# The last feature tiles in slices of 384 and 128 tokens, the closing norm applied over four tiles at a time

## The chip, the cores and the metric

The kernel runs on one core of a Trainium2 chip. The metric is device time in microseconds (us), the median of three runs. Lower is better.

## What is computed

Two transformer-like blocks over 512 tokens and 1024 features. Only the last step matters here, the second convolutional feed-forward of the second block, whose output passes a root-mean-square norm and is added to the residual:

```python
def rms_norm(x, g):
    xf = x.astype(jnp.float32)
    y = xf * lax.rsqrt(jnp.mean(xf * xf, axis=-1, keepdims=True) + EPS)
    return (y * g.astype(jnp.float32)).astype(x.dtype)
...
def conv_ffn(h, w_up, w_conv, b_conv, w_down):
    g, u = jnp.split(h @ w_up, 2, axis=-1)
    g = causal_dwconv(g, w_conv) + b_conv.astype(g.dtype)
    return (jax.nn.silu(g) * u) @ w_down
...
        x = x + rms_norm(conv_ffn(h, w_up[layer], w_ffn_conv[layer], b_ffn_conv[layer], w_down[layer]),
                         norm_g[layer, 3])
```

## The kernel before

Features lie on the 128 partitions, tokens along the free axis, so the residual is eight feature tiles `X[0]` to `X[7]` of 128x512. Each float32 product is made of three matmuls in the fp32r format (`mm3`, lines 175 to 177): a high and a low part of the weights (`whi`, `wlo`) against a high and a low part of the activations (`mh`, `ml`). `wload` brings a block of weights of up to 1024 columns by DMA into `raw`, ScalarE makes `whi` of it (line 137), VectorE makes `wlo` as the difference (line 144). There are three buffers of each.

The down projection of a feed-forward is done by `finish`: for each of the eight output tiles 22 blocks of weights, so 66 matmuls and three weight loads (1024, 1024 and 768 columns). Tiles 0 to 5 are done over all 512 tokens. The last `split` tiles (two here, 6 and 7) are done in two slices of tokens, `HALVES`: tiles 6 and 7 for tokens 0 to 255, then tiles 7 and 6 for tokens 256 to 511. The weights of tile 7 are kept for the second slice, those of tile 6 are loaded and split again. After each tile `evac` multiplies the result by a per-token factor `R` into `mix` (line 476, VectorE) and collects its squares (`stat`): ScalarE squares, VectorE adds to `acc` (lines 265 and 266); the last tile of a slice goes another way, its squares (line 255) are summed on TensorE directly (`sums`, line 283, one matmul for every 128 tokens).

After each slice comes `after(c)`, that is `post`: `rnorm` makes the factor of the norm from the sums in small operations (lines 298 to 305; the square root needs a table load on ScalarE), spreads it over the partitions by matmuls into PSUM (line 308), and then for each of the eight feature tiles one VectorE operation multiplies `mix` by the norm's weight and factor (line 383), one adds it to the residual (line 385; in the last slice four of the eight adds are on GpSimd), and SyncE issues the output's DMA (line 394). The first slice's `post` lies beside the second slice's matmuls, the second one's is the end of the kernel.

The order of the instructions on each engine is settled when the program is built. Engines work through their own list in order and wait on each other by semaphores. TensorE's weight loads (PEld) run beside its matmuls.

Of the kernel before, what the change touches and what calls it, by code (L numbers as in the profile page):

```python
# [9 lines left out]
F32 = mybir.dt.float32  # L10
F32R = mybir.dt.float32r
AF = mybir.ActivationFunctionType
ALU = mybir.AluOpType
# [3 lines left out]
P = 128  # L17
S = 512
D = 1024
KD = D // P  # L20
# [12 lines left out]
HALVES = (slice(0, S // 2), slice(S // 2, S))  # L33
# [16 lines left out]
class Net:  # L50
# [164 lines left out]
        for (key, _), p in zip(tiles, ps):  # L215
            self.ready[key] = p

    def finish(self, src, acts, split, evac, after, pool=None):


        K = len(acts)
        n = KD - split
        for m in range(n):
            evac(m, self.proj(src[m], acts, "mo"[m % 2], key=("out", m)), WHOLE)
        if not split:
            return after(WHOLE)
        alloc = None
        if pool is not None:
            alloc = lambda: [[pool.tile([P, 1024], F32R, name=nm, tag="w", bufs=2 * split)] for nm in ("oh", "ol")]
        chunks = [range(k0, min(K, k0 + 8)) for k0 in range(0, K, 8)]  # L230
        load = lambda m: [self.wload(src[m][:, ks[0] * P : ks.stop * P], alloc) for ks in chunks]
        w = {m: load(m) for m in range(n, KD)} if pool is not None else {}
        i = 0
        for c in HALVES:
            ms = range(n, KD) if c.start == 0 else range(KD - 1, n - 1, -1)
            for m in ms:
                wm = w[m] if m in w else load(m)
                if m == KD - 1:
                    w[m] = wm
                ps = self.psum("mo"[i % 2])[:, 0 : S // 2]  # L240
                i += 1
                for ks, wc in zip([self.order] if self.order else chunks, wm):
                    self.mmk(ps, wc, acts, ks, c, ks[0] if self.order else 0, ks[-1] if self.order else K - 1)
                evac(m, ps, c, m == ms[-1])
            after(c)


    def stat(self, t, c, first, of="x", direct=False):

        nc = self.nc  # L250
        if direct:
            sq = self.tp.tile([P, S // 2], F32, name="sq", tag="sq", bufs=2)
            for h in HALVES:
                if c.start <= h.start < c.stop:
                    nc.scalar.activation(sq, t[:, h], AF.Square)
                    self.sums(sq, h, c, of)
            return
        if first and c.start == 0:
            self.acc[of] = self.tp.tile([P, S], F32, name="acc", tag="acc", bufs=1)
        acc = self.acc[of]  # L260
        if first:
            nc.scalar.activation(acc[:, c], t[:, c], AF.Square)
        else:
            sq = self.tmp("sq")
            nc.scalar.activation(sq[:, c], t[:, c], AF.Square)
            nc.vector.tensor_tensor(out=acc[:, c], in0=acc[:, c], in1=sq[:, c], op=ALU.add)
# [110 lines left out]
    def post(self, mix, gname, g0, nxt, c):  # L377

        nc = self.nc
        R = self.rnorm("mix", D, None, c)  # L380
        for k in range(KD):
            t = mix[k][:, c]
            nc.vector.scalar_tensor_tensor(t, t, self.vec(gname, g0 + k), R[:, c], ALU.mult, ALU.mult)
            eng = nc.gpsimd if nxt[0] == "end" and c.stop == S and k < 6 and k % 3 < 2 else nc.vector
            eng.tensor_tensor(out=self.X[k][:, c], in0=self.X[k][:, c], in1=t, op=ALU.add)
            if nxt[0] == "normed":
                if k % 2:
                    self.stat2(self.X[k - 1 : k + 1], c)
            elif nxt[0] == "scaled":
                if k == 0 and c.start == 0:  # L390
                    self.alloc_h()
                self.h_scaled(nxt, k, c)
            else:
                nc.sync.dma_start(self.out[k][:, c], self.X[k][:, c])
        if nxt[0] == "scaled":
            for k in range(0, KD, 2):
                self.stat2(self.X[k : k + 2], c)

    def first_begin(self, tiles, allocs):

# [22 lines left out]
    def ffn(self, up, down, nxt, conv=None, post=None, extra=None):  # L423
        nc, tc = self.nc, self.tc
        with tc.tile_pool(name="mida", bufs=KD) as sa, tc.tile_pool(name="mid", bufs=2 * KF - KD) as sp:
            with tc.tile_pool(name="ft", bufs=2) as fp:
                part = lambda nm: [sp.tile([P, S], F32R, name=nm, tag="s") for _ in range(2)]
                tiles = [((up.tensor.name, i), up[i]) for i in range(6)]
                allocs = [lambda: (part("bh"), part("bl"))] * 3
                if self.early:  # L430
                    self.begin(tiles, allocs)
                else:
                    self.first_begin(tiles, allocs)
                    self.early = True
                R = self.R
                if conv is not None:
                    pads = [fp.tile([P, S + 2], F32, name=f"pad{i}", bufs=1) for i in range(2)]
                    for t in pads:
                        nc.gpsimd.memset(t[:, 0:2], 0.0)
                mids = []  # L440
                h = self.H
                for j in range(KF):
                    pg = self.proj(up[2 * j], h, "m", key=(up.tensor.name, 2 * j))
                    pu = self.proj(up[2 * j + 1], h, "o", key=(up.tensor.name, 2 * j + 1))
                    gp = fp.tile([P, S], F32, name="gp", tag="gp")
                    if conv is None:
                        nc.vector.tensor_tensor(out=gp, in0=pg, in1=R, op=ALU.mult)
                    else:
                        wn, bn, l = conv
                        pad = pads[j % 2]  # L450
                        nc.vector.tensor_tensor(out=pad[:, 2:], in0=pg, in1=R, op=ALU.mult)
                        w = lambda t: self.vec(wn, (l * 3 + t) * KF + j)
                        nc.scalar.activation(gp, pad[:, 2:], AF.Identity, bias=self.vec(bn, l * KF + j), scale=w(2))
                        nc.vector.scalar_tensor_tensor(gp, pad[:, 1 : S + 1], w(1), gp, ALU.mult, ALU.add)
                        nc.vector.scalar_tensor_tensor(gp, pad[:, 0:S], w(0), gp, ALU.mult, ALU.add)
                    nc.scalar.activation(gp, gp, AF.Silu)
                    md = fp.tile([P, S], F32, name="md", tag="md")
                    nc.vector.tensor_tensor(out=md, in0=pu, in1=gp, op=ALU.mult)  # L458
                    mids.append(self.split(sa if j < KD // 2 else sp, md, "s", "m"))
                    if extra is not None:  # L460
                        gen, steps = extra
                        for _ in range(steps * (j + 1) // KF - steps * j // KF):
                            next(gen, None)
            with tc.tile_pool(name="fm", bufs=KD) as mp:
                mix = {}

                def evac(m, ps, c, last=False):
                    if post is None:
                        t = self.tmp("dx")
                        nc.vector.scalar_tensor_tensor(t[:, c], ps, 0.5, R[:, c], ALU.mult, ALU.mult)  # L470
                        nc.vector.tensor_tensor(out=self.X[m][:, c], in0=self.X[m][:, c], in1=t[:, c], op=ALU.add)
                        self.updated(nxt, m, c, last)
                    else:
                        if m not in mix:
                            mix[m] = mp.tile([P, S], F32, name="mix", tag="mix")
                        nc.vector.tensor_tensor(out=mix[m][:, c], in0=ps, in1=R[:, c], op=ALU.mult)
                        self.stat(mix[m], c, m == 0, "mix", last)

                def after(c):
                    if post is not None:  # L480
                        self.post(mix, *post, nxt, c)
                    self.prep(nxt, c)

                self.finish(down, mids, 3 if nxt[0] == "normed" else 2, evac, after)


    def attention(self, ap, Q, K, V, blocks, step, logits, out, mask=None, lag=1, bank=None):
# [843 lines left out]
```

## Time and profile before

| | |
|---|---|
| median of 3 runs (2466.15 to 2467.6) | 2467.29 us |
| the profiled execution's own time | 2469.19 us |
| its span | 2467.4 us |
| TensorE busy | 2403.5 us, 97% of the span |
| VectorE, ScalarE, GpSimd busy | 1468.1, 1129.9, 39.1 us |
| mean granted TensorE clock | 0.992 of full speed |

The profile is of one execution, whose span is 1.8 us shorter than its own time. A row of windows gives a stretch (start:end, its length), then the busy time and the number of instructions (x) of PE, PEld, DVE, ACT and POOL, the granted TensorE clock as a share of full speed, and the DMA engines' share and rate. Names in rows are those of the program, with buffer numbers left out. PE is TensorE's matmuls, PEld its weight loads, DVE VectorE, ACT ScalarE, POOL GpSimd, SPq the DMA queue of SyncE.

### The profile page before, as it was taken

How to read it: one execution, taken by the hardware profiler on the slowest of the kernel's cores; microseconds unless marked ns; L12 is line 12 of the kernel's file. 1: busy time of each engine (PE TensorE's matmuls, PEld its weight loads, DVE VectorE, ACT ScalarE, POOL GpSimd, SP SyncE). 2: the span in 40 equal slices, each digit the busy share in tenths (PEclk: the TensorE clock that was granted, in tenths of full speed). 3: DMA queues.
4: the chain of work that ended last, by engine and by line, in shares of the span. 5: the costliest groups of instructions: out<-in, count | busy, mean ns of one | idle time of the engine just before them, and what ended most of it. 6: DMA issues, size and time to landing. Idle time of an engine off the chain costs nothing.

```text
span 2467.4 us, 32211 instructions
## 1 busy us (share of the span) xinstructions
PE 2403.5 (97%) x12710; PEld 2048.5 (83%) x12710; DVE 1468.1 (60%) x2524; ACT 1129.9 (46%) x1849; POOL 39.1 (2%) x75
## 2 busy tenths in 40 slices
PE   9999999999999999999999999999999979999998
PEld 8888898777777798888988798888898859888887
DVE  5444347888888755553556665554357996555524
ACT  5223236766666544442355554333246566433322
POOL 0000000000000000000000000000001120000000
PEclk9999999999999999999999999999999999999999
DMA  4232333322222256663432222322344413223233
GB/s 151 94 102 92 94 112 119 95 88 88 80 99 84 86 204 213 214 227 95 117 118 82 85 94 69 102 95 90 101 151 150 145 53 136 69 97 101 90 96 94
DMA packets 83559, 276.08 MB, mean 112 GB/s; under 512 B 9328, under 2 KB 14064, under 8 KB 83408
## 3 DMA queue, kind: packets, MB, share of 16 engines
q1 hardware_dynamic: 83408, 274.03, 34.4%
q8 instruction: 99, 1.62, 0.3%
q14 instruction: 52, 0.43, 0.1%
HBM read 257.20 MB, written 16.80 MB: 111 GB/s over the span
## 4 chain that ended last, share of the span: by engine, by line
PE 84%; DVE 9%; ACT 4%; issue 2%; DMA 1%; POOL 0%; SPq 0%; ACTq 0%; DVEq 0%; POOLq 0%
PE psm L177 15%; PE psm L175 15%; PE psm L176 15%; PE pso L176 10%; PE pso L175 10%; PE pso L177 10%; DVE wlo L144 1%; DVE pso L1063 1%; ACT whi L137 1%; PE pst L516 1%; PE pso L532 1%; PE pst L175 1%; PE pst L176 1%; PE pst L283 1%; PE pst L177 1%
## 5 line engine op out<-in xcount | busy, mean ns | idle before, releaser
L137 ACT CAST whi<-raw 128x1024 fp32r<-128x1024 f32 (+3 forms) x402 | 408.5, 1017 | 770.3 <-issue 340.3
L144 DVE TENSOR_TENSOR wlo<-raw,whi 128x1024 fp32r<-128x1024 f32 (+2 forms) x380 | 447.7, 1179 | 311.0 <-ACT whi L137 309.9
L175 PE MATMUL psm<-hh,whi 128*128 128x512 f32 (+1 forms) x1512 | 573.2, 380 | 4.2 <-ACT hh L326 3.0
L177 PE MATMUL psm<-hl,whi 128*128 128x512 f32 (+1 forms) x1512 | 569.0, 377 | 0.1
L176 PE MATMUL psm<-hh,wlo 128*128 128x512 f32 (+1 forms) x1512 | 569.0, 376 | 0.0
L175 PEld LDWEIGHTS psm<-hh,whi 128*128 128x128 f32 x1512 | 285.7, 189 | 54.1 <-ACT hh L326 3.9
L177 PEld LDWEIGHTS psm<-hl,whi 128*128 128x128 f32 x1512 | 285.7, 189 | 49.7 <-DVE hl L327 0.7
L176 PEld LDWEIGHTS psm<-hh,wlo 128*128 128x128 f32 x1512 | 286.2, 189 | 46.5
L175 PE MATMUL pso<-hh,whi 128*128 128x512 f32 (+1 forms) x728 | 272.8, 375 | 0.9 <-ACT whi L137 0.9
L176 PE MATMUL pso<-hh,wlo 128*128 128x512 f32 (+1 forms) x728 | 272.4, 374 | 0.2 <-DVE wlo L144 0.2
L177 PE MATMUL pso<-hl,whi 128*128 128x512 f32 (+1 forms) x728 | 272.5, 374 | 0.0
L176 PE MATMUL psm<-mh,wlo 128*128 128x512 f32 (+1 forms) x506 | 172.5, 341 | 1.6 <-DVE wlo L144 1.6
L175 PE MATMUL psm<-mh,whi 128*128 128x512 f32 (+1 forms) x506 | 172.1, 340 | 0.0
L177 PE MATMUL psm<-ml,whi 128*128 128x512 f32 (+1 forms) x506 | 172.0, 340 | 0.0
L458 DVE TENSOR_TENSOR md<-pso,gp 128x512 f32<-128x512 f32 x84 | 58.0, 692 | 169.7 <-PE pso L177 168.2
L175 PEld LDWEIGHTS pso<-hh,whi 128*128 128x128 f32 x728 | 137.9, 189 | 25.1 <-ACT whi L137 1.1
L176 PEld LDWEIGHTS pso<-hh,wlo 128*128 128x128 f32 x728 | 137.9, 189 | 24.3 <-DVE wlo L144 0.4
L177 PEld LDWEIGHTS pso<-hl,whi 128*128 128x128 f32 x728 | 137.8, 189 | 24.5 <-issue 0.5
L176 PE MATMUL pso<-mh,wlo 128*128 128x256 f32 (+1 forms) x440 | 145.7, 331 | 1.3 <-DVE wlo L144 1.3
L175 PE MATMUL pso<-mh,whi 128*128 128x256 f32 (+1 forms) x440 | 145.9, 332 | 0.3 <-ACT whi L137 0.3
L177 PE MATMUL pso<-ml,whi 128*128 128x256 f32 (+1 forms) x440 | 145.8, 331 | 0.0
L176 PEld LDWEIGHTS psm<-mh,wlo 128*128 128x128 f32 x506 | 96.8, 191 | 12.6 <-DVE wlo L144 2.2
(293 smaller groups left out, 3763.5 us busy)
## 6 DMA issues: line engine op xcount, KB each, us to landing
raw<-w_up SPq DMA_DIRECT2D x88, 512.0 KB, 3.3
raw<-w_ffn_gu SPq DMA_DIRECT2D x87, 512.0 KB, 3.4
raw<-w_in SPq DMA_DIRECT2D x56, 512.0 KB, 3.3
raw<-w_ffn_down SPq DMA_DIRECT2D x40, 512.0 KB, 3.5
raw<-w_in_odd SPq DMA_DIRECT2D x40, 512.0 KB, 3.9
raw<-w_down SPq DMA_DIRECT2D x38, 512.0 KB, 3.5
raw<-w_in_even SPq DMA_DIRECT2D x24, 512.0 KB, 3.6
w_in_odd_lo<-raw SPq DMA_DIRECT2D x20, 512.0 KB, 3.0
```

What stands on the lines that cost most here:

```text
L137: nc.scalar.copy(hi, raw[:, c])
L144: nc.vector.tensor_tensor(out=lo, in0=raw[:, c], in1=hi.bitcast(F32), op=ALU.subtract)
L175: nc.tensor.matmul(out, w[0], x[0], start=start, stop=False)
L176: nc.tensor.matmul(out, w[1], x[0], start=False, stop=False)
L177: nc.tensor.matmul(out, w[0], x[1], start=False, stop=stop)
L283: self.nc.tensor.matmul(st[:, b : b + 1], sq[:, i * P : (i + 1) * P], self.ones[:, 0:1], start=new and i == 0, stop=True, skip_group_check ...
L458: nc.vector.tensor_tensor(out=md, in0=pu, in1=gp, op=ALU.mult)
L516: nc.tensor.transpose(pt[:, i * P : (i + 1) * P], p[:, i * P : (i + 1) * P], self.ident)
L532: nc.tensor.matmul(o[:, q0:q1], V[:, g, a].rearrange("p i d -> p (i d)"), p[:, c], start=first, stop=g == 3 and p is pl, skip_group_check= ...
L1063: nc.vector.scalar_tensor_tensor(t, pad[:, i : i + S], w(i), t, ALU.mult, ALU.add)
```

## The change

For the last feed-forward alone (`end`), the two slices become tokens 0 to 383 and 384 to 511. `mix` becomes one tile `MA` of 128x8x512, so that an operation can run over four feature tiles. The norm's weight is multiplied in by ScalarE right after a tile's squares are taken, and `post_end` takes the place of `post`: for each group of four tiles one multiplication by the norm's factor, one addition to the residual, and one output transfer, all on VectorE and SyncE.

```diff
-    def finish(self, src, acts, split, evac, after, pool=None):
+    def finish(self, src, acts, split, evac, after, pool=None, cuts=HALVES):
...
-        for c in HALVES:
+        for c in cuts:
...
-                ps = self.psum("mo"[i % 2])[:, 0 : S // 2]
+                ps = self.psum("mo"[i % 2])[:, 0 : c.stop - c.start]
...
-            for h in HALVES:
-                if c.start <= h.start < c.stop:
-                    nc.scalar.activation(sq, t[:, h], AF.Square)
-                    self.sums(sq, h, c, of)
+            for h in (slice(a, min(a + S // 2, c.stop)) for a in range(c.start, c.stop, S // 2)):
+                nc.scalar.activation(sq[:, : h.stop - h.start], t[:, h], AF.Square)
+                self.sums(sq, h, c, of)
...
-            eng = nc.gpsimd if nxt[0] == "end" and c.stop == S and k < 6 and k % 3 < 2 else nc.vector
-            eng.tensor_tensor(out=self.X[k][:, c], in0=self.X[k][:, c], in1=t, op=ALU.add)
+            nc.vector.tensor_tensor(out=self.X[k][:, c], in0=self.X[k][:, c], in1=t, op=ALU.add)
...
-            else:
-                nc.sync.dma_start(self.out[k][:, c], self.X[k][:, c])
...
+    def post_end(self, mix, c):
+
+        nc = self.nc
+        n = c.stop - c.start
+        R = self.rnorm("mix", D, None, c)[:, c].rearrange("p (k s) -> p k s", k=1).to_broadcast([P, 4, n])
+        out = self.out.rearrange("k p s -> p k s")
+        for k in range(0, KD, 4):
+            t, x = (a[:, k : k + 4, c] for a in (mix, self.XA))
+            nc.vector.tensor_tensor(out=t, in0=t, in1=R, op=ALU.mult)
+            nc.vector.tensor_tensor(out=x, in0=x, in1=t, op=ALU.add)
+            nc.sync.dma_start(out[:, k : k + 4, c], x)
...
+                        nc.vector.tensor_tensor(out=t[:, c], in0=ps, in1=R[:, c], op=ALU.mult)
+                        self.stat(t, c, m == 0, "mix", last)
+                        if end:
+                            nc.scalar.activation(t[:, c], t[:, c], AF.Copy, scale=self.vec(post[0], post[1] + m))
...
+                cuts = (slice(0, 3 * P), slice(3 * P, S)) if end else HALVES
+                self.finish(down, mids, 3 if nxt[0] == "normed" else 2, evac, after, cuts=cuts)
```

Ahead of the last feed-forward's down projection the order of instructions is the same on every engine. Three places show what moves.

The first is VectorE's list from the last step of the first slice's norm factor (`r`) to the last `wlo` of the second slice. Before:

```order
L305 SCALAR_TENSOR_TENSOR r<-y,r 128x2 [waits DVE_49]
L144 TENSOR_TENSOR wlo<-raw,whi 128x1024 [waits DMAHW3_49,Activation_49]
L383 SCALAR_TENSOR_TENSOR mix<-mix,vecs,pst 128x256 [waits PE_49]
L383 SCALAR_TENSOR_TENSOR mix<-mix,vecs,pst 128x256
L385 TENSOR_TENSOR x<-x,mix 128x256 [waits DVE_49] x2
...
L476 TENSOR_TENSOR mix<-psm,R 128x256 [waits PE_49]
L144 TENSOR_TENSOR wlo<-raw,whi 128x1024 [waits DMAHW4_49,Activation_49]
L266 TENSOR_TENSOR acc<-acc,sq 128x256 [waits Activation_49]
L144 TENSOR_TENSOR wlo<-raw,whi 128x768 [waits DMAHW5_49]
```

The same stretch of the change:

```order
L304 SCALAR_TENSOR_TENSOR r<-y,r 128x3 [waits DVE_49]
L403 TENSOR_TENSOR mix<-mix,pst 128x4x384 [waits PE_49]
L403 TENSOR_TENSOR mix<-mix,pst 128x4x384
L404 TENSOR_TENSOR x<-x,mix 128x4x384 [waits DVE_49] x2
L144 TENSOR_TENSOR wlo<-raw,whi 128x1024 [waits DMAHW3_49,Activation_49]
L144 TENSOR_TENSOR wlo<-raw,whi 128x1024 [waits DMAHW4_49,Activation_49]
L486 TENSOR_TENSOR mix<-psm,R 128x128 [waits PE_49]
L144 TENSOR_TENSOR wlo<-raw,whi 128x768 [waits DMAHW5_49,Activation_49]
```

Sixteen operations of 256 tokens (the dots stand for twelve of them) become four of 4x384, and the first `wlo` for tile 6 of the second slice stood ahead of them and now stands behind them.

The second is ScalarE's list from the square of the first slice's last tile to the first `whi` of tile 6 in the second slice. Before:

```order
L255 ACTIVATE sq<-mix 128x256 [waits DVE_49]
L299 ACT_TABLE_LOAD
L299 ACTIVATE u<-pst,epst 128x2 [waits DVE_49]
L137 CAST whi<-raw 128x1024 [waits DMAHW3_49,PE_49,Activation_49]
```

The same stretch of the change:

```order
L254 ACTIVATE sq<-mix 128x256 [waits DVE_49]
L254 ACTIVATE sq<-mix 128x128 [waits PE_49]
L489 ACTIVATE mix<-mix,vecs 128x384 [waits Activation_49]
L298 ACT_TABLE_LOAD
L298 ACTIVATE u<-pst,epst 128x3 [waits DVE_49]
L137 CAST whi<-raw 128x1024 [waits DMAHW3_49,PE_49]
```

A second square, which waits for TensorE to have read the first out of the same buffer, and the multiplication by the norm's weight now stand ahead of the table load.

The third is VectorE's list behind the last tile of the kernel. Of the change, from the first step of the norm factor on:

```order
L297 TENSOR_SCALAR v<-pst 128x1 [waits PE_49]
L299 RECIPROCAL r<-u 128x1 [waits Activation_49]
L303 SCALAR_TENSOR_TENSOR y<-r,v 128x1 [waits DVE_49]
L304 SCALAR_TENSOR_TENSOR r<-y,r 128x1 [waits DVE_49]
L403 TENSOR_TENSOR mix<-mix,pst 128x4x128 [waits PE_49]
L403 TENSOR_TENSOR mix<-mix,pst 128x4x128
L404 TENSOR_TENSOR x<-x,mix 128x4x128 [waits DVE_49] x2
```

Before, eight multiplications and four additions of 128x256 stood there on VectorE, with four additions on GpSimd, and two operations `y` in place of the one. On TensorE the 66 matmuls of a tile stay 66, of 384 columns in the first slice and of 128 in the second.

## Rows read from the trace of the kernel before

**Rows 1.** The page, first part: busy time (share) and instructions; fourth part: chain by engine.
```profile
PE 2403.5 (97%) x12710; PEld 2048.5 (83%) x12710; DVE 1468.1 (60%) x2524; ACT 1129.9 (46%) x1849; POOL 39.1 (2%) x75
...
PE 84%; DVE 9%; ACT 4%; issue 2%; DMA 1%; POOL 0%; SPq 0%; ACTq 0%; DVEq 0%; POOLq 0%
```
**Rows 2.** Busy time by windows: first slice, second slice, what follows the last matmul.
```profile
2420.38:2436.21 15.83, 15.83 (x134) 15.83 (x132) 6.33 (x8) 4.62 (x6) 0.00 (x0) 1.00 0.47 145
2436.21:2455.21 19.00, 17.74 (x146) 17.24 (x144) 10.98 (x27) 5.31 (x7) 0.00 (x0) 1.00 0.17 57
...
2455.21:2467.40 12.19, 1.74 (x12) 1.49 (x12) 6.30 (x18) 0.68 (x2) 2.96 (x4) 0.69 0.26 86
```
**Rows 3.** Timeline (start, us, what): fp32r matmuls of 384 columns, four in a row.
```profile
490.47 0.34 PE L532 MATMUL pso<-ph,v 128*128 128x384 f32 x1
...
491.00 0.34 PE L532 MATMUL pso<-pl,v 128*128 128x384 f32 x1
```
**Rows 4.** Timeline: fp32r matmuls of 128 columns and their weight loads, one after another.
```profile
1917.88 0.22 PE L532 MATMUL pso<-ph,v 128*128 128x128 f32 x1
...
1917.94 0.27 PE L532 MATMUL pso<-pl,v 128*128 128x128 f32 x1
1917.99 0.19 PEld L502 LDWEIGHTS pst<-kh,qs 128*128 128x128 f32 x1
1918.05 0.28 PE L502 MATMUL pst<-kh,qs 128*128 128x128 f32 x1
...
1918.33 0.19 PEld L175 LDWEIGHTS psm<-hh,whi 128*128 128x128 f32 x1
```
**Rows 5.** Chain of waits, then timeline: VectorE in the second slice, TensorE's stall.
```profile
2442.68 0.78 DVE mix L383 x2
2443.47 0.67 DVE x L385 x2
...
2448.84 1.14 DVE wlo L144
...
2450.02 0.39 PE L176 MATMUL pso<-mh,wlo 128*128 128x256 f32 x1 [1.25 <-DVE wlo L144]
```
**Rows 6.** Timeline: VectorE's evacuation of 512 tokens, ScalarE behind the first slice.
```profile
2420.58 0.69 DVE L476 TENSOR_TENSOR mix<-pso,R 128x512 f32<-128x512 f32 x1 [1.73 <-PE pso L177]
...
2436.87 0.42 ACT L255 ACTIVATE sq<-mix 128x256 f32<-128x256 f32 x1 [7.22 <-DVE mix L476]
2437.30 1.28 ACT L299 ACT_TABLE_LOAD   x1
```
**Rows 7.** Chain of waits behind the last matmul (start, us, what).
```profile
2455.24 0.43 DVE mix L476
...
2456.16 1.07 PE pst L283 x8
...
2457.94 0.36 DVE y L304 x2
...
2458.64 0.70 PE pst L308 x4
2459.36 1.66 DVE mix L383 x4
...
2464.01 0.42 DVE x L385
```
**Rows 8.** DMA issues: count, KB each, median us from issue to landing.
```profile
raw<-lru_w SPq DMA_DIRECT2D x8, 256.0 KB, 2.7
...
out<-x SPq DMA_DIRECT2D x16, 128.0 KB, 1.8
```
**Rows 9.** TensorE's timeline at an earlier norm, and the window behind it.
```profile
1490.63 0.61 PE L283 MATMUL pst<-ones,sq 128*128 128x1 f32 x4 [1.20 <-DVE sq L273]
1492.66 0.68 PE L308 MATMUL pst<-spread,r 128*128 128x128 f32 x4 [1.42 <-DVE r L305]
...
1494.00:1497.40 3.40, 3.40 (x18) 3.40 (x17) 3.05 (x5) 2.80 (x3) 0.00 (x0) 0.51 0.02 6
```

More of the change, by code (lines that the diff above doesn't have):

```diff
@@ L463, in ffn @@
                             next(gen, None)
-            with tc.tile_pool(name="fm", bufs=KD) as mp:
-                mix = {}
+            with tc.tile_pool(name="fm", bufs=1) as mp:
+                end = nxt[0] == "end"
+                if post is not None:
+                    MA = mp.tile([P, KD, S], F32, name="mix")
+                    mix = [MA[:, m, :] for m in range(KD)]
                 def evac(m, ps, c, last=False):
@@ L473, in evac @@
                     else:
[L474 to L477, printed above, removed]
+                        t = mix[m]
+                        nc.vector.tensor_tensor(out=t[:, c], in0=ps, in1=R[:, c], op=ALU.mult)
+                        self.stat(t, c, m == 0, "mix", last)
+                        if end:
+                            nc.scalar.activation(t[:, c], t[:, c], AF.Copy, scale=self.vec(post[0], post[1] + m))
                 def after(c):
+                    if end:
+                        return self.post_end(MA, c)
                     if post is not None:
@@ L482, in after @@
                     self.prep(nxt, c)
-                self.finish(down, mids, 3 if nxt[0] == "normed" else 2, evac, after)
+                cuts = (slice(0, 3 * P), slice(3 * P, S)) if end else HALVES
+                self.finish(down, mids, 3 if nxt[0] == "normed" else 2, evac, after, cuts=cuts)
     def attention(self, ap, Q, K, V, blocks, step, logits, out, mask=None, lag=1, bank=None):
```

## Prediction

> **What bounds the kernel now.** I read the page first: TensorE is busy for 97% of the span and carries 84% of the chain that ended last [rows 1], so whatever TensorE takes longer for goes into the time unless it was waiting anyway. Then the end, by windows [rows 2]. The first slice takes 15.83 us for its 132 matmuls of 256 columns, 0.120 us each, with TensorE never idle. The second takes 19.00 us from its first matmul to the end of its last: 15.84 us of matmuls at that rate, some 1.4 us of the norm's small ones (twelve between the matmuls), and a stall of 1.25 us, in which TensorE waits for a `wlo` that stands behind the first slice's norm on VectorE [rows 5]. From there to the end of the span are 12.19 us, a chain of short steps on VectorE, ScalarE and TensorE, 5.07 us of norm and residual (2459.36 to 2464.43) and 2.97 us of output transfer [rows 7, 2]. So the change touches three stretches: two bound by TensorE, one by latency. I take them in turn, and call F the start of the second slice.
>
> **First slice, 256 to 384 columns.** Four fp32r matmuls of 384 columns with a weight load each start 0.53 us apart over three gaps, 0.173 to 0.180 us each with the rounding of the starts [rows 3]; I take 0.175. 132 of them are 23.1 us, against 15.83: **+7.3 us**. Nothing hides it, since TensorE has no idle time there.
>
> **Second slice, 256 to 128 columns.** A matmul is not cheaper in proportion. Among matmuls of 128 columns, one whose weights were loaded early starts 0.06 us after the one before it (1917.88 to 1917.94), but the next comes 0.11 later, and the weight loads of such a run follow each other at (1918.33 - 1917.99)/3 = 0.113 us [rows 4]. In a steady run the weight load sets the pace, because every matmul has its own. The bounds are 0.06 and 0.113; I take 0.113, the row of a run. So the second slice's matmuls come to 132 x 0.113 = 14.9 us, only 0.9 less than now: the columns saved here do not pay for those added in the first slice.
>
> The Trainium skill, "TensorE: Matmul & The Clock Gate", section on the back-to-back issue gap, gives about 81 ns per matmul for a stream of weight loads and matmuls of 128 columns. No run here shows that figure; the measured 0.113 is higher. By the page's figure the 65 matmuls that count below would take 2.1 us less, and the sum would be so much lower, still a loss.
>
> But matmuls are not all that sets this slice. The steps, each from its start: the evacuation of 384 tokens begins at F+0.20 as now and takes 0.56 us (half way between 0.43 for 256 and 0.69 for 512 [rows 7, 6]); the square of 256 tokens 0.42 [rows 6], to F+1.2; two sums on TensorE, which the second square must wait for, some 0.6; that square of 128 tokens about 0.32 (between half of 0.42 and all of it), to F+2.2; then on ScalarE the multiplication by the norm's weight, 0.53 (between 0.42 and 0.63 if it goes by the columns), and the table load of 1.28 [rows 6], to F+4.05. Before, the table load stood right behind the square and was hidden by the sums. Square root, reciprocal, three `y` at 0.18 and the last step take the factor to F+5.3 and its spreading on TensorE, six matmul instructions at 0.113 plus the wait for the last, to F+6.35. TensorE has work for part of that: 21 matmuls stand ahead of the spreading, and some 1.6 us are waits.
>
> Now VectorE runs the four wide operations, and the first `wlo` of tile 6 behind them. An operation on 256 tokens costs 0.39 us at line 383 and 0.335 at line 385 [rows 5], and 256 more tokens 0.26 more (0.69 less 0.43). 1536 elements are six such parts: 0.39 + 5 x 0.26 = 1.69 and 1.64, for four 6.65 us. Bounds: 6.2 if only the slope counts, 8.7 if each part pays its full price; I take 6.65, since the 512-token row shows the slope. They end at F+13.0, and the `wlo` (1.14 [rows 5]) at F+14.2. TensorE has done the other 45 matmuls of tile 7 by F+11.2 and one of tile 6, then waits **3.0 us**, against 1.25 now. From there 65 matmuls at 0.113 take 7.4 us, and the next two `wlo`, due at F+15.3 and about F+16.5, come before they are needed at F+16.9 and F+19.6. The last evacuation starts at F+21.75, against F+19.03: **+2.7 us**.
>
> **The clock.** The rows of an earlier norm show what such waits can do: TensorE was idle 1.20 and then 1.42 us within some three us, and the granted clock of the next 3.4 us was 0.51 [rows 9], which is the lower of its levels (1.2 against 2.4 GHz). In the second slice of before, with one wait of 1.25 us, it stayed at 1.00 [rows 2]. A wait of 3.0 us is longer than both together, so I expect one fall as long as that. While it lasts the work goes at half speed, so 3.4 us cost up to 1.7; part falls into the wait itself. I take **+1.4 us**, with bounds of 0 (no fall) and about 4.5 (half speed for most of tile 6 and of the small matmuls behind it).
>
> **What follows the last matmul.** Evacuation -0.13 (half the slope), square -0.10, sums four instructions instead of eight, -0.5 of 1.07, one `y` instead of two -0.18, spreading two instead of four -0.23 of 0.70 [rows 7]. The norm and residual: four operations of 512 elements, 0.65 and 0.60 each, 2.5 us instead of 5.07: -2.55. In sum -3.7. The last transfer is 256 KB instead of 128: the nearest rows are 2.7 and 1.8 us to landing [rows 8], +0.9 (from 0, if only the latency counts, to 1.8, if it queues behind its twin, issued 0.6 us earlier). **-2.8 us**, between -3.7 and -1.9.
>
> ScalarE's eight multiplications by the norm's weight cost nothing ahead of the slices: it is busy 4.62 of 15.83 us in the first slice [rows 2]. Uncovered, each would cost up to 0.6. GpSimd's four adds go without loss, since they lay beside VectorE's. No weight load is queued behind the wide transfers: all are issued before.
>
> **Sum.** 7.3 + 2.7 + 1.4 - 2.8 = +8.6 us. The profiled execution would go from a span of 2467.4 to 2476.0, and its time from 2469.19 to 2477.8; that execution is 1.9 us above the median of the runs, 2467.29, which becomes **2475.9**, 0.35% slower. A measurement of this kernel tells differences from about 0.2%, 4.9 us.
>
> **The rivals.**
> - *The clock holds.* Same mechanism without the fall: +7.2, 2474.5. For it: it stayed up over the wait of 1.25 us. Against it: what followed a little less idle time than 3.0 us in [rows 9]. 0.25.
> - *The clock stays low for longer,* because of the 1.6 us of waits ahead of the spreading and of matmuls that start every 0.113 us where 0.06 would do: +10 to +12, about 2478.5. For it: the second slice holds 4.6 us of waits, all told. Against: between them TensorE has work. 0.15.
> - *Weight loads hide (the other side).* If a run of 128-column matmuls goes at the 0.06 us of the pair in [rows 4], the 65 behind the wait take 3.9 instead of 7.4, and with the clock up the sum is +3.7: 2471.0, within 0.2%. It decides below about 0.078 us each with the clock up. For it: that pair. Against: the spacing of the weight loads just behind it. 0.10.
> - *Wide operations are cheap.* If VectorE does 4x384 in half of 1.65 us, the wait and the fall go: 7.2 - 3.0 = +4.2, 2471.5, also within 0.2%. It decides from about 4.3 us for all four. For it: fewer starts. Against: 0.26 us for each 256 more elements. 0.06.
> - *Faster by over 0.2%* would need both, and more from the transfer. 0.02.
>
> **How the numbers follow.** Forecast 0.42, with its own range 2474.8 to 2477.5. Slower by over 0.2%: 0.42 + 0.25 + 0.15 = 0.82; within 0.2%: 0.16; faster: 0.02. The range from 2471.2 to 2479.5 takes in the bounds of the wide operations (up to +2.0), of the transfer (0.9 either way) and of the clock, and leaves out the case in which the weight loads hide and the far end of a long fall.
>
> **What the changed kernel's profile would show.** Gaps of 0.175 us between matmuls of 384 columns, a first slice of 23.1 us; 0.113 between those of 128; 4x384 operations of some 1.65 us; a wait of about 3 us of tile 6's first `wlo` matmul for VectorE; a granted clock of 0.5 behind it; 9.4 us from the last matmul to the end. I would be wrong if matmuls of 128 columns run at about 0.06, or the wait on `wlo` is gone.

## The result, and the profile after

The changed kernel takes **2485.02 us** (median of 6 runs, 2482.06 to 2486.71) against 2467.48 for the kernel before, measured beside it (2466.15 to 2468.55). The ratio is 1.0070, with a 95% interval from 1.0059 to 1.0081: 0.7% slower, by about twice what was predicted. The profiled execution took 2485.19 us, with a span of 2483.1.

The page first. These are its lines of busy time and of the chain by engine, which answer to [rows 1]:

```profile
PE 2423.7 (98%) x12710; PEld 2068.2 (83%) x12710; DVE 1467.1 (59%) x2504; ACT 1136.3 (46%) x1860; POOL 35.9 (1%) x71
...
PE 84%; DVE 8%; ACT 4%; issue 2%; DMA 1%; POOL 0%; SPq 0%; POOLq 0%; DVEq 0%; ACTq 0%
```

TensorE issues the same 12710 matmuls as before and is busy for 20.2 us longer. The work has not grown in instructions, so single instructions must have become longer. The first slice's wider matmuls account for 7.1 us of it (22.91 below against 15.83 in [rows 2]).

The same stretches as in [rows 2], by windows (stretch, length, busy time and instructions of PE, PEld, DVE, ACT and POOL, granted clock, DMA share, GB/s): first slice, second slice, the part of the second slice from 2448.85 on, and what follows the last matmul.

```profile
2420.12:2443.03 22.91, 22.91 (x134) 22.91 (x133) 6.69 (x8) 6.07 (x8) 0.00 (x0) 1.00 0.34 100
2443.03:2473.11 30.08, 28.89 (x151) 28.41 (x150) 12.02 (x17) 6.42 (x10) 0.00 (x0) 0.60 0.15 53
...
2448.85:2473.11 24.26, 24.22 (x115) 24.03 (x113) 10.48 (x10) 3.53 (x5) 0.00 (x0) 0.50 0.18 66
...
2473.11:2483.10 9.99, 1.78 (x6) 1.43 (x6) 3.48 (x9) 0.97 (x3) 0.00 (x0) 0.50 0.19 52
```

Against [rows 2] the first slice takes 7.1 us more, the second 11.1 more, and the end 2.2 less. With 0.3 less ahead of them, that is the 15.7 us by which the span grew. The second slice stands out, and the column of the granted clock says why: 1.00 there before, 0.60 now, and 0.50 from 2448.85 to its end. 0.50 is the lower of TensorE's two levels, 1.2 GHz. Once there, the clock did not come back in 24 us, although TensorE was busy for 24.22 of those 24.26.

TensorE's timeline around the fall (start, time, instruction, with the wait before it and its releaser in brackets):

```profile
2443.42 0.28 PE L176 MATMUL psm<-mh,wlo 128*128 128x128 f32 x1
2443.53 0.27 PE L177 MATMUL psm<-ml,whi 128*128 128x128 f32 x1
2444.28 0.61 PE L282 MATMUL pst<-ones,sq 128*128 128x1 f32 x4 [0.48 <-ACT sq L254]
...
2445.07 0.38 PE L282 MATMUL pst<-ones,sq 128*128 128x1 f32 x2
2445.31 0.81 PE L282 MATMUL pst<-ones,acc 128*128 128x1 f32 x6
...
2448.30 1.19 PE L307 MATMUL pst<-spread,r 128*128 128x128 f32 x6 [0.67 <-DVE r L304]
...
2450.04 0.41 PE L176 MATMUL psm<-mh,wlo 128*128 128x128 f32 x1
2450.25 0.41 PE L177 MATMUL psm<-ml,whi 128*128 128x128 f32 x1
```

Before the fall two matmuls start 0.11 us apart, behind it 0.21. Between them stand two waits for the first slice's norm, 0.48 and 0.67 us, and the norm's own matmuls: twelve sums of a single column each, and six instructions that spread the factor. The wait on `wlo` that the prediction expected, 3.0 us, is missing. VectorE's timeline shows that it is not VectorE that became faster:

```profile
2449.53 3.42 DVE L403 TENSOR_TENSOR mix<-mix,pst 128x1536 f32<-128x1536 f32 x2 [1.38 <-PE pst L307]
2452.87 3.42 DVE L404 TENSOR_TENSOR x<-x,mix 128x1536 f32<-128x1536 f32 x2
2456.20 2.35 DVE L144 TENSOR_TENSOR wlo<-raw,whi 128x1024 fp32r<-128x1024 f32 x2
```

The four wide operations take 6.84 us (6.65 predicted), and the `wlo` behind them is as late as expected. TensorE no longer waits for it because TensorE itself is late: at 0.21 us a matmul it has not finished tile 7 when the first `wlo` ends.

The chain of waits behind the last matmul, which answers to [rows 7], and from VectorE's timeline its last two operations:

```profile
2473.11 0.30 DVE mix L486
...
2473.79 1.03 PE pst L282 x4
...
2475.53 0.23 DVE y L303
...
2476.09 0.78 PE pst L307 x2
...
2476.89 1.28 DVE mix L403 x2
2478.18 0.60 DVE x L404
...
2478.10 1.29 DVE L404 TENSOR_TENSOR x<-x,mix 128x512 f32<-128x512 f32 x2
```

Norm and residual take 2.5 us (2476.89 to 2479.39) instead of 5.07, as the sum had it. But four sums on TensorE take 1.03 us where eight took 1.07, and two spreading instructions 0.78 where four took 0.70: the clock is at 0.50 here too.

### The profile page after: what moved, and what is told of

It reads as the page before. It is cut to its first block, busy times and chain, and to the rows that moved or that the text cites. A ratio compares the mean times of both kernels' runs of the same rounds, so it can differ in the third digit from the quotient of the medians.

```text
span 2483.1 us, 32175 instructions
## 1 busy us (share of the span) xinstructions
PE 2423.7 (98%) x12710; PEld 2068.2 (83%) x12710; DVE 1467.1 (59%) x2504; ACT 1136.3 (46%) x1860; POOL 35.9 (1%) x71
## 4 chain that ended last, share of the span: by engine, by line
PE 84%; DVE 8%; ACT 4%; issue 2%; DMA 1%; POOL 0%; SPq 0%; POOLq 0%; DVEq 0%; ACTq 0%
PE psm L177 15%; PE psm L175 15%; PE psm L176 15%; PE pso L175 10%; PE pso L176 10%; PE pso L177 10%; PE pso L548 1%; ACT whi L137 1%; DVE wlo L144 1%; DVE pso L1079 1%; PE pst L532 1%; PE pst L282 1%; PE pst L175 1%; PE pst L176 1%; PE pst L177 1%
## 5 line engine op out<-in xcount | busy, mean ns | idle before, releaser
L176 PE MATMUL psm<-mh,wlo 128*128 128x512 f32 (+3 forms) x506 | 175.5, 347 | 1.6 <-DVE wlo L144 1.6
L175 PE MATMUL psm<-mh,whi 128*128 128x512 f32 (+3 forms) x506 | 174.9, 346 | 0.0
L177 PE MATMUL psm<-ml,whi 128*128 128x512 f32 (+3 forms) x506 | 174.9, 346 | 0.0
L175 PE MATMUL pso<-mh,whi 128*128 128x256 f32 (+3 forms) x440 | 149.9, 341 | 0.3 <-ACT whi L137 0.3
L177 PE MATMUL pso<-ml,whi 128*128 128x256 f32 (+3 forms) x440 | 149.7, 340 | 0.0
L176 PE MATMUL pso<-mh,wlo 128*128 128x256 f32 (+3 forms) x440 | 149.5, 340 | 0.0
```

What stands on the lines that cost most here:

```text
L175: nc.tensor.matmul(out, w[0], x[0], start=start, stop=False)
L176: nc.tensor.matmul(out, w[1], x[0], start=False, stop=False)
L177: nc.tensor.matmul(out, w[0], x[1], start=False, stop=stop)
```

## The experiments

The theory after the result, which the expectations call C, is that the clock carries the loss. In a stream of matmuls of 128 columns the norm of the first slice, with its short waits, brings the clock down, and the stream then does not bring it back. The rivals blame the new norm itself (its wide operations and the waits for them, whatever the width of the matmuls), or a 128-column stream that is slow by itself. Two rounds of four kernels were run. The kernel before took 2467.99 us (median) beside the first round (e1, e2, e4, e5) and 2467.73 beside the second. All edits are to the changed kernel.

**e1_halves: the slices back at 256 tokens, all else as changed.**

```diff
-                cuts = (slice(0, 3 * P), slice(3 * P, S)) if end else HALVES
+                cuts = HALVES
```

> Slices of 256 and 256 tokens as before, with everything else of the change: the norm over four tiles, ScalarE's multiplication, two transfers a slice. Theory C (the columns: TensorE's clock falls after the waits at the start of the second slice, and matmuls of 128 columns, which at the lower clock start 0.213 us apart, don't bring it back): the clock stays at 1.00 over the second slice or is back after 3.4 us, the slice takes 19 to 20 us, and the time is 2465 to 2470 us. Rival N (the loss is the norm's new form, its wide operations and larger transfers): 2480 us or more, with long waits in the second slice. Rival W (the waits alone keep the clock low, whatever the columns): the clock at 0.5 over most of the second slice, about 2478 us.

Measured: 2468.09 us, ratio 0.9999 (0.9990 to 1.0008). Windows of its first slice, second slice and end, then two rows of the end (the spreading, and the last two operations):

```profile
2419.08:2434.91 15.83, 15.83 (x133) 15.83 (x132) 6.33 (x8) 5.85 (x8) 0.00 (x0) 1.00 0.47 144
...
2434.90:2452.57 17.67, 17.66 (x146) 17.23 (x144) 9.69 (x15) 6.34 (x9) 0.00 (x0) 1.00 0.18 61
...
2452.57:2466.30 13.73, 2.25 (x12) 1.90 (x12) 5.88 (x10) 1.19 (x3) 0.00 (x0) 0.59 0.23 76
...
2455.99 1.21 PE pst L307 x4
...
2459.49 2.35 DVE L404 TENSOR_TENSOR x<-x,mix 128x1024 f32<-128x1024 f32 x2
```

The whole loss is in the cut: with the new norm and equal slices the time is that of before. The windows also show what the new norm does when left alone. TensorE's stall of 1.25 us [rows 5] is gone (17.66 of 17.67 us busy), and the second slice is 1.3 us shorter than before, also shorter than the 19 to 20 us expected. The end is 1.5 us longer than before: norm and residual are a little shorter (2457.22 to 2461.84, 4.6 us against 5.07), but the last transfer takes 4.5 us instead of 2.97, and the spreading, at the low clock, 1.21 instead of 0.70. A gain and a loss of nearly one size cancel.

**e2_oldnorm: the uneven slices with the old norm** (per-tile operations, additions on GpSimd, eight transfers a slice, no multiplication on ScalarE).

```diff
...
-            nc.vector.tensor_tensor(out=self.X[k][:, c], in0=self.X[k][:, c], in1=t, op=ALU.add)
+            eng = nc.gpsimd if nxt[0] == "end" and c.stop == S and k < 6 and k % 3 < 2 else nc.vector
+            eng.tensor_tensor(out=self.X[k][:, c], in0=self.X[k][:, c], in1=t, op=ALU.add)
...
-                        if end:
-                            nc.scalar.activation(t[:, c], t[:, c], AF.Copy, scale=self.vec(post[0], post[1] + m))
...
-                    if end:
-                        return self.post_end(MA, c)
```

> Slices of 384 and 128 tokens, with the norm as before: one multiplication, one addition and one transfer for each feature tile, GpSimd's adds in the last slice. Theory C: as the change, the clock at 0.5 over most of the second slice, 2482 to 2488 us. Rival N: near the kernel before, 2467 to 2471 us. Rival W: the clock is back once the first slice's norm is done, about 2476 us.

Measured: 2484.25 us, ratio 1.0066 (1.0052 to 1.0080), within 0.8 us of the change. TensorE's first wait in its second slice, then windows of the start and the rest of that slice:

```profile
2441.65 0.61 PE L282 MATMUL pst<-ones,sq 128*128 128x1 f32 x4 [0.48 <-ACT sq L254]
```

```profile
2440.39:2443.33 2.94, 2.46 (x21) 2.28 (x20) 0.56 (x1) 1.66 (x3) 0.00 (x0) 0.99 0.00 0
2443.33:2471.45 28.12, 28.08 (x132) 27.89 (x131) 12.55 (x27) 3.84 (x6) 0.00 (x0) 0.50 0.16 57
```

The new norm is not the cause. The same low clock follows, here 1.7 us behind the start of the sums that had waited 0.48 us, and stays for 28 us, to the end of the slice. Up to the fall that wait is the only one: 2.46 of 2.94 us are busy.

**e4_no_waits: the uneven slices without the first slice's norm.** Its last sums and its application are left out, and the residual goes out as it is.

```diff
-                        self.stat(t, c, m == 0, "mix", last)
+                        if not (end and m > 5 and c.start == 0):
+                            self.stat(t, c, m == 0, "mix", last)
...
+                    if end and c.start == 0:
+                        return nc.sync.dma_start(self.out.rearrange("k p s -> p k s")[:, :, c], self.XA[:, :, c])
```

> The change without the first slice's norm: its two last tiles' squares, the factor, the norm and the addition to the residual are left out, and the residual goes out as it is for those 384 tokens. So nothing makes TensorE wait at the start of the second slice, and its 132 matmuls of 128 columns come one after another at full clock. If the columns alone are enough to lose the clock (C in its strong form): it falls in the second slice though nothing waits, and the slice takes more than 18 us. If waits are needed for the fall (C in its weak form, and W): the clock stays at 1.00, the matmuls start 0.113 us apart, and the slice takes 14.9 us.

Measured: 2468.83 us, ratio 1.0003 (0.9994 to 1.0012). The window of its second slice:

```profile
2443.26:2458.15 14.89, 14.85 (x133) 14.71 (x132) 4.37 (x7) 4.16 (x6) 0.00 (x0) 1.00 0.01 2
```

132 matmuls of 128 columns at the full clock, 0.113 us each, for 15 us on end. So a stream of 128 columns did not bring the clock down by itself; the norm had to interrupt it. Two things went with the norm, though: its waits, and its matmuls of a single column on TensorE. No run takes away one and keeps the other among matmuls of 128 columns, so which of them brings the clock down is not shown. The window also confirms the 14.9 us of the prediction. And it bounds what the cut could be worth: with the first slice's norm left out and the clock up, the kernel is no faster than before. (Its end holds a table load of 1.28 us that the omitted norm would have taken; less that, it would by estimate stand near 2467.5, still no gain.)

**e5_dense: the second slice's matmuls over 256 columns** (the 128 before the slice are computed again and not used), so that TensorE has double the columns and the same number of instructions.

```diff
+                cc = slice(min(c.start, S // 2), c.stop)
...
-                    self.mmk(ps, wc, acts, ks, c, ks[0] if self.order else 0, ks[-1] if self.order else K - 1)
-                evac(m, ps, c, m == ms[-1])
+                    self.mmk(ps, wc, acts, ks, cc, ks[0] if self.order else 0, ks[-1] if self.order else K - 1)
+                evac(m, ps[:, c.start - cc.start :], c, m == ms[-1])
```

> The change, with the second slice's matmuls over 256 columns instead of 128: tokens 256 to 383 of tiles 7 and 6 are computed a second time and not used, so the same instructions do twice the columns. Theory C: the clock falls once after the waits and is back within 3.4 or 6.8 us, since a 256-column matmul keeps the array in use; the second slice takes 21 to 24 us instead of 30, and the time is 2474 to 2479 us, 6 to 10 less than the change, though TensorE has more to do. Rival W: the clock stays at 0.5, the matmuls start 0.213 us apart as in the change, and the time is that of the change, 2485 us.

Measured: 2474.18 us, ratio 1.0028 (1.0017 to 1.0038): **11 us less than the change, with twice the columns in that slice.** Its one wait, and two matmuls behind the fall:

```profile
2458.16 0.38 PE L176 MATMUL pso<-mh,wlo 128*128 128x256 f32 x1 [1.83 <-DVE wlo L144]
...
2460.50 0.41 PE L177 MATMUL pso<-ml,whi 128*128 128x256 f32 x1
2460.72 0.41 PE L175 MATMUL pso<-mh,whi 128*128 128x256 f32 x1
```

Windows of the second slice, of its part ahead of the wait, and of the stretch around the low clock:

```profile
2443.10:2464.85 21.75, 19.88 (x151) 19.36 (x150) 11.93 (x17) 6.53 (x10) 0.00 (x0) 0.92 0.21 73
...
2443.10:2456.05 12.95, 12.95 (x109) 12.83 (x109) 8.80 (x12) 5.82 (x8) 0.00 (x0) 1.00 0.01 1
...
2459.50:2459.75 0.25, 0.25 (x4) 0.25 (x4) 0.00 (x0) 0.00 (x0) 0.00 (x0) 0.94 0.99 350
2459.75:2463.00 3.25, 3.25 (x17) 3.25 (x17) 0.00 (x0) 0.00 (x0) 0.00 (x0) 0.50 0.20 70
2463.00:2463.25 0.25, 0.25 (x4) 0.25 (x3) 0.00 (x0) 0.00 (x0) 0.00 (x0) 0.73 0.00 0
```

The clock passes the norm at its upper level, falls behind the wait of 1.83 us for `wlo`, and is back after some 3.4 us. This is the fall that the prediction had in mind, for matmuls of another width. At the low clock 256 columns start 0.21 to 0.22 us apart, as 128 do. The run does not show that 256 columns would stand the norm's waits, since it has none: with the wider matmuls the built order changes, ten matmuls instead of six stand ahead of the first sums, and TensorE is busy for all of the 12.95 us ahead of the `wlo` wait. VectorE's order changes too: the first `wlo` stands ahead of the wide operations, and the wait is for the second. So some of the 11 us may belong to the order and not to the width.

**e5b_dense_late: 256 columns in tile 6 only**, the second tile of the slice (`if m == KD - 2`, and `c.start` otherwise), and **e5c_dense_early: in tile 7 only**, the first (`if m == KD - 1`).

```diff
+                cc = slice(min(c.start, S // 2) if m == KD - 2 else c.start, c.stop)
```

> The change, with 256 columns instead of 128 for tile 6 alone, the last 66 matmuls of the kernel (128 columns of them computed a second time and not used). Theory C: the clock falls in tile 7 as in the change, tile 7's matmuls start 0.213 us apart to their end, and within tile 6 the clock comes back after 3.4 to 6.8 us, the matmuls then starting 0.12 us apart: 3 to 5 us less than the change, 2480 to 2482 us. Rival W (once the clock has fallen there, it stays low whatever the columns): 0.213 us to the end, 2484 to 2486 us.

> The mirror image: 256 columns for tile 7 of the second slice, 128 for tile 6. Up to the wait of 1.8 us for tile 6's second wlo it should go as the run with 256 columns for both, the clock at 1.00. Behind that wait 42 matmuls are left. Theory C: the clock falls there as it did in that run, but with 128 columns it doesn't come back, so they start 0.213 us apart where those of 256 columns were back at 0.12 after 3.4 us: 2 to 4 us more than that run, 2476 to 2478 us, though TensorE has fewer columns to do. Rival W: the same or a little less than that run, 2472 to 2474.5 us.

e5b_dense_late took 2480.53 us, ratio 1.0051 (1.0037 to 1.0064). It keeps the change's order up to the end of tile 7, with the wait of 0.48 us, and the clock falls at the last of the sums, at 2444.0. Windows from there to the end of tile 7 (128 columns), at the start of tile 6 (256 columns), and in the rest of it:

```profile
2444.00:2457.71 13.71, 13.71 (x67) 13.71 (x66) 10.00 (x12) 3.34 (x4) 0.00 (x0) 0.50 0.24 87
2457.71:2461.01 3.30, 3.30 (x16) 3.30 (x17) 1.45 (x3) 1.45 (x3) 0.00 (x0) 0.50 0.34 122
2461.01:2467.20 6.19, 6.19 (x52) 6.09 (x51) 0.00 (x0) 0.00 (x0) 0.00 (x0) 1.00 0.00 0
```

Through 13.7 us of 128-column matmuls the clock stays at 0.50, with TensorE busy without a gap. The wider matmuls behind them start no further apart (16 in 3.30 us), and after 3.3 us of them the clock is at 1.00. TensorE is busy throughout both stretches, so what differs ahead of the rise is the width of the matmuls and not idle time.

e5c_dense_early took 2476.96 us, ratio 1.0040 (1.0025 to 1.0056). Its wait in tile 6 (for the second `wlo`, in the order of e5_dense), then windows from the start of the slice to that wait's end (tile 7 with 256 columns, and what of tile 6 could run before the wait) and of tile 6 behind the fall (128 columns):

```profile
2456.60 0.33 PE L176 MATMUL pso<-mh,wlo 128*128 128x128 f32 x1 [2.08 <-DVE wlo L144]
```

```profile
2441.51:2456.50 14.99, 13.00 (x110) 12.74 (x109) 10.81 (x15) 6.55 (x10) 0.00 (x0) 1.00 0.14 49
...
2458.21:2465.20 6.99, 6.66 (x32) 6.47 (x31) 0.29 (x1) 0.00 (x0) 0.00 (x0) 0.50 0.09 31
```

In tile 7 the clock holds; it falls behind the wait on `wlo`, and the 128-column matmuls of tile 6 stay at 0.50. It computes fewer columns than e5_dense and takes 2.8 us more. This run also shows a wait of the predicted kind, 2.1 us long, where the clock lets TensorE get that far.

**e3_small_first: 128 tokens first, 384 last.**

```diff
-                cuts = (slice(0, 3 * P), slice(3 * P, S)) if end else HALVES
+                cuts = (slice(0, P), slice(P, S)) if end else HALVES
```

> The change with the slices the other way round, 128 tokens first and then 384. The 132 matmuls of 128 columns now follow dense work and nothing makes them wait. Theory C in its weak form (waits are needed for the fall): the clock stays at 1.00 in the first slice, which takes 14.9 us, the second takes 24 to 25 us, and what follows the last matmul is 4 to 6 us longer than before because 384 tokens are left for it: 2474 to 2480 us. If a run of 128 columns loses the clock without a wait: more than 18 us in the first slice and 2482 us or more.

Measured: 2477.54 us, ratio 1.0041 (1.0027 to 1.0055). Windows of first slice, second slice and end:

```profile
2418.20:2432.89 14.69, 14.69 (x134) 14.69 (x132) 6.07 (x8) 5.64 (x8) 0.00 (x0) 1.00 0.51 157
2432.89:2456.77 23.88, 23.87 (x140) 23.44 (x139) 7.83 (x14) 6.25 (x9) 0.00 (x0) 1.00 0.08 23
...
2456.77:2474.90 18.13, 3.28 (x18) 2.84 (x18) 8.29 (x11) 1.61 (x4) 0.00 (x0) 0.62 0.24 87
```

Nothing interrupts the 128-column slice here, and it runs at 1.00. What the uneven cut costs without any fall can be read from the two slices: 14.69 + 23.88 = 38.6 us, against 34.8 in [rows 2], 3.7 more. The end is longer by 5.9 us, because three quarters of the tokens now pass through it. Together that is nearly the 9.8 us by which the median is longer.

**e6_wide_first: halves, the wide norm for the first slice only, the old one for the last.** This was the attempt at a faster kernel: the stall of [rows 5] away, the end as before. The old norm's lines are those of e2_oldnorm and are left out here.

```diff
...
                         if end:
-                            nc.scalar.activation(t[:, c], t[:, c], AF.Copy, scale=self.vec(post[0], post[1] + m))
+                            if c.start == 0:
+                                q = slice(0, S // 2)
+                                nc.scalar.activation(t[:, q], t[:, q], AF.Copy, scale=self.vec(post[0], post[1] + m))
...
-                    if end:
+                    if end and c.start == 0:
                         return self.post_end(MA, c)
...
-                cuts = (slice(0, 3 * P), slice(3 * P, S)) if end else HALVES
+                cuts = HALVES
```

> Slices of 256 and 256, the new norm over four tiles for the first slice, the old one (eight transfers, four adds on GpSimd) for the last. The wait of 1.25 us before the second wlo of tile 6 goes, because four operations of 4x256 take 4.7 us on VectorE instead of 6; what follows the last matmul is as before, 12.2 us. Theory C and N alike: 1 to 1.5 us less than before, 2466 to 2467 us, at the edge of what can be told. If the wait was hidden work anyway: no difference.

Measured: 2467.88 us, ratio 0.9999 (0.9990 to 1.0007). Windows of the second slice and the end:

```profile
2436.43:2454.13 17.70, 17.66 (x146) 17.23 (x144) 9.70 (x16) 5.83 (x8) 0.00 (x0) 1.00 0.18 61
2454.13:2466.70 12.57, 2.25 (x12) 1.90 (x12) 6.30 (x18) 0.68 (x2) 2.95 (x4) 0.60 0.25 83
```

The stall is gone, 1.3 us off the second slice. The end is 0.4 us longer, with more of TensorE's time in it (2.25 us against 1.74) at a lower clock. The 1 to 1.5 us that were expected did not show: what is left of the gain is below what the runs can tell, and no kernel here is shown to be faster than the one before.

## Why the prediction was half right

**First slice: right.** +7.3 predicted, +7.1 measured; 132 matmuls in 22.91 us are 0.174 each, against 0.175 from [rows 3].

**The price of 128 columns: right at the full clock, and only there.** 0.113 us each, from the weight loads in [rows 4], is what e4_no_waits shows over a whole slice; e3_small_first shows 0.111. The rival in which weight loads hide (0.06) fell.

**The clock: this is the step that failed.** "I expect one fall as long as that", taken at +1.4 us with a bound of 4.5, rested on [rows 9]. There the clock was back after 3.4 us, and I carried that duration over to a stream of another width. The runs show two things in its place.
- *The fall stays.* In matmuls of 128 columns the clock did not return: 24 us in the change, 28 in e2_oldnorm, 13.7 in e5b_dense_late until the columns became 256, and back 3.3 us later. The prediction asked how long a fall lasts and not what would end it.
- *It comes from less.* I looked for it behind the 3.0 us wait on `wlo`. It came some 6 us into the slice, behind waits of 0.48 and 0.67 us and the norm's sums, and in e2_oldnorm and e5b_dense_late behind the first wait and the sums alone. The 1.25 us of [rows 5], with 256 columns around them, had not done it; 1.83 us in e5_dense did. e4_no_waits shows that without the norm's interruptions there is no fall.

The size follows from the rows. At the low clock a matmul starts every 0.213 us instead of 0.113, and 111 of the slice's 132 do: 11.1 us. That this is just the growth of the second slice is partly chance: the narrower matmuls save 0.9 us at the full clock, and the waits and the norm's own matmuls take 0.9 us more than before (30.08 less 26.0 of matmuls, against 19.00 less 15.84). The slower sums and spreading at the end are 0.8 more: 1.03 + 0.78 us, where the prediction had 0.57 + 0.47.

Why a 128-column matmul takes 0.213 there can be read in part. The row of a weight load in the change at the low clock (PEld is TensorE's weight loads; [rows 4] has 0.19 at the full one):

```profile
2450.15 0.33 PEld L177 LDWEIGHTS psm<-ml,whi 128*128 128x128 f32 x1
```

The loads follow each other 0.21 us apart, as the matmuls do. Matmuls of 256 columns go at the same distance in e5_dense and e5b_dense_late. What both widths have is a weight load of 128 columns for each matmul, so for 128 columns it is probably again the weight load that sets the pace, at half its speed; that is worked out from these rows and was not tested by itself. The Trainium skill, "TensorE: Matmul & The Clock Gate", section on LDWEIGHTS, gives a load as its columns divided by 1.2, in ns, with no word of the clock's state; for 128 columns that is 107 ns. As an estimate from that figure, 111 matmuls paced by their loads would take 11.9 us at either level, and a fall would cost such a stream nothing. The trace comes near it at the full clock (113 ns) and not at the low one (213 ns).

**Second slice's wait: did not come, for a reason that lies in the step above.** Of +2.7 us, 1.75 was the wait on `wlo` that grew from 1.25 to 3.0. VectorE was as late as predicted (6.84 us for the wide operations). With the clock at 0.50 TensorE was later still, and the wait turned into slow matmuls. Where the clock held through tile 7 a wait of that kind was there, for the second `wlo`: 1.83 us in e5_dense, 2.08 in e5c_dense_early. In the place of +2.7 and +1.4 stands the measured +11.1.

**The end: right in kind, -2.8 predicted, -2.2 measured.** Norm and residual went from 5.07 to 2.5 us, and the transfer from 2.97 to 3.7, both as the sum had them. Of the difference of 0.6 us the clock's slower sums and spreading take 0.8, and the other steps came out 0.2 better.

**The rival "the clock stays low for longer"** is what happened, and it was mis-sized: 2478.5 against 2485.02. It named the right place, the short waits ahead of the spreading in a stream of 128 columns, but its +10 to +12 is about what the clock's bound of 4.5 gives (7.2 + 4.5 = 11.7), half speed for most of tile 6; the fall covered 45 matmuls of tile 7 and all of tile 6. The forecast sum of +8.6 us against a measured 15.7 lacks 7.1; the second slice lacks 11.1 - 2.7 - 1.4 = 7.0 of it.

What stays open: which part of the norm starts the fall in the change, one of the two short waits or the sums of a single column between them. They stand within some four us of each other, and no run took away one alone. Among matmuls of 256 columns the norm's sums did not bring the clock down (e1_halves, e5_dense), but there TensorE did not wait at the norm either.

## What to carry to other kernels

A price per matmul holds for one level of TensorE's clock: before narrowing a stream of matmuls, ask what would bring the clock back once it has fallen, and look for rows of the same width to answer that, since here the clock came back behind some 3 us of 256 columns and not in 28 us of 128. Narrow slices next to a norm, or next to a wait for weights as in e5c_dense_early, are therefore risky beyond their own price, and recomputing columns that nobody needs was 4.5 us cheaper than leaving them out for one tile (e5b_dense_late) and 11 us for both (e5_dense, with another order). Where each matmul has its own weight load, cutting tokens unevenly costs by itself (38.6 against 34.8 us for the two slices of e3_small_first, with no fall), and what it takes from the end must first pay for that.

## What the hardware showed unexpectedly

A busy TensorE can sit at the low clock: in the change it was busy 24.22 of 24.26 us at 0.50. The same stream of 128 columns held 1.00 for 14.89 us when nothing interrupted it (e4_no_waits), so in these runs the level depended on what came before. And at 0.50 matmuls of 128 and of 256 columns start the same 0.21 us apart, so the wider ones cost no time there.
